# Value products of the grouped-query entry in three groups of tiles, and two weight splits pinned to other instructions

## The chip, the core and the metric

The kernel runs on one core of one Trainium2 chip. The metric is the device time of one execution in microseconds (us). A core has a matrix engine (TensorE, PE in the profile; PEld is its loading of weights), a vector engine (VectorE, DVE), an engine for activation functions (ScalarE, ACT), a general one (GpSimd, POOL) and one that only issues transfers (SyncE, SP). Each works through its own list of instructions in order; they wait for each other by semaphores. PE writes its products into PSUM, a memory of eight banks of 128 x 512 fp32 words; DVE and ACT read them from there into SBUF, the working memory. GpSimd doesn't read PSUM in this kernel.

## What is computed

One inference step of a two-layer diffusion backbone of width 1024, for 512 latent tokens and 128 context tokens that share all weights. The 640 tokens go through both layers side by side. Layer 0 has latent attention heads and neighbourhood attention heads, layer 1 has grouped-query attention; each is followed by a gated feed-forward block. The change lies at the start of layer 1's attention. Cut to what matters there:

```
def odd_project(h, w_in, q_norm, k_norm):
    p = h @ w_in
    q, k, v = jnp.split(p, [GQA_HEADS * GQA_HEAD_DIM, (GQA_HEADS + GQA_KV_HEADS) * GQA_HEAD_DIM], axis=-1)
    q = rms_norm(q.reshape(b, L, GQA_HEADS, GQA_HEAD_DIM), q_norm)
    k = rms_norm(k.reshape(b, L, GQA_KV_HEADS, GQA_HEAD_DIM), k_norm)
    ...
def odd_mixer_latent(h, c_k, c_v, w_in, q_norm, k_norm, w_out, cos, sin):
    q, k, v = odd_project(h, w_in, q_norm, k_norm)
    q = apply_rope(q, cos, sin)
    k = apply_rope(k, cos, sin)
    o = attend_blocked(q, jnp.concatenate([k, c_k], axis=1), jnp.concatenate([v, c_v], axis=1), GQA_SCALE)
    return o.reshape(b, L, -1) @ w_out
```

There are 8 query heads and 2 key/value heads of 128 columns each. The latent tokens read their own 512 keys and values and 128 cached ones; the context tokens read only themselves. Everything is fp32.

## The kernel before

**Precision and splits.** Every operand of a product is kept as two parts, a high part in PE's reduced fp32 form and a low part, the rest; a product is three matmuls (high x high, high x low, low x high). A weight of 128 x 1024 words is therefore loaded from memory into a raw buffer (three in turn) and split into one of three weight buffers: ACT copies the high part (line 184) and DVE subtracts it from the raw words to give the low part (line 185). The function is `unit` (line 175); its argument `behind` holds back ACT's half, DVE's half or both until a given instruction of the same engine has been issued. Names: wgk0 and wgk1 are the weights of the two key heads, wgv0 and wgv1 those of the values (the first and the second half of the 1024 inputs, for both heads), wgq0 to wgq7 those of the query heads; a trailing r is the raw buffer.

**Tokens and tiles.** The 640 tokens lie along the free dimension in two halves of 320 for keys and queries. For the values they are cut into five tiles of 128 tokens, each a product of 128 x 256 words (both value heads). The layer's input is h10 (h10h and h10l, its high and low part), eight blocks of 128 features.

**The entry.** Key head 0, query head 0 and the values are projected while the input is still being made block by block. `gvalues(ts, ks)` (line 1831) does the value products of the tiles `ts` for the feature blocks `ks`, the blocks in the outer loop, the tiles in the inner. The five tiles gvo[0] to gvo[4] lie in three PSUM banks, gvp0 to gvp2: tiles 0 and 1 in the first, 2 and 3 in the second, 4 in the third. The second half (line 2006) does all five tiles for blocks 4 to 7. Behind it, line 2011 splits each value tile and the tile of cached values cvf into gvh (ACT) and gvl (DVE); `valued` keeps the pair of instructions of the split that was written last. Line 2013 copies the context tokens' values to gvf, which GpSimd stores as an output. Then the second half of query head 0 is projected, and line 2016 closes the PSUM pool of the value banks and opens the one for the scores (`open_y(s=2)`, two tiles of two banks each).

**The heads.** For each query head the code builds named pieces and runs them in an order that is written out by hand. For head 0:

```
GQA_FIRST = "s0 x0 k0 k1 s1 r k2 k3 s2 k4 k5 s3 k6 k7 s4 q0 q1 q2 q3 q4 q5 q6 q7"
```

s0 to s4 are the score products (gs) of the five blocks of 128 queries, with the row maximum (gn) on DVE; x0 is the weighing of s0 (in the others it is part of the piece): a small product gb on DVE (line 1950), the Exp on ACT (line 1951), a reciprocal on DVE and the division on GpSimd (line 376). k0 to k7 are the products of key head 1 (gk1a, gk1b), r the query norms of head 0, q0 to q7 the query products of head 1. Each query product is followed by a copy out of PSUM (gqc), a square (gsq), a rotation on DVE (gqr, lines 1821 to 1824) and a split (gqh, gql).

**The order on each engine.** The order of the pieces fixes PE's order. The other engines' order is fixed by a planner of the framework when the program is built: it runs the program through estimates of its own and gives an engine that is free the next instruction that can start, by the order of the code where there are several. So an instruction that stands late in the code can run early, as wgq1's split does in the profile of before; `behind` is the code's means against that. Line 1894 pins head 1's query weights behind `valued[0]`, which in this version is the split of the cached tile.

Of the kernel before, what the change touches and what calls it, by code (L numbers as in the profile page):

```python
# [13 lines left out]
AF = mybir.ActivationFunctionType  # L14
ALU = mybir.AluOpType
# [5 lines left out]
KT = D // P  # L21
# [29 lines left out]
def body(ctx, tc, xT, vecs, crow, wm0, wm0g, wm1, wA, wNV, wNA, wMK, wMV, wOA, wGQ, wGK, wGV, wOC,  # L51
# [3 lines left out]
    V, S, G = nc.vector, nc.scalar, nc.gpsimd  # L55
# [32 lines left out]
    def bank(name, kind="m"):  # L88
        if kind == "m":
            return psp.tile([P, 512], F32, tag="m", bufs=4, name=name)  # L90
        return ypool["pool"].tile([P, 512], F32, tag=kind, bufs=ypool["tags"][kind], name=name)
# [10 lines left out]
    def tmp(name):  # L102
        return tp.tile([P, T], F32, tag="t", bufs=3, name=name)

    def f(ap):
        return ap.bitcast(F32)
# [41 lines left out]
    def vcol(i):  # L148
        return vec[:, i:i + 1]
# [12 lines left out]
    def load(src, n, name):  # L162
        raw = rawp.tile([P, 1024], F32, tag="raw", name=name)
        nc.sync.dma_start(raw[:, :n], src)
        return raw[:, :n]

    def after(inst, fn):
        if inst is None:
            return fn()
        with tc.issue_after(inst.ins):  # L170
            return fn()
# [3 lines left out]
    def unit(src, n, name, lo="v", pool=None, behind=None, raw=None):  # L175

        if raw is None:
            raw = load(src, n, name + "r")
        else:
            nc.sync.dma_start(raw, src)  # L180
        t = (pool or wp).tile([P, 2, 1024], F32R, tag="w", bufs=3, name=name)
        hi, lw = t[:, 0, :n], t[:, 1, :n]
        at = behind if isinstance(behind, tuple) else (behind, behind)
        split[:] = (after(at[0], lambda: S.activation(hi, raw, AF.Copy)),
                    after(at[1], lambda: (V if lo == "v" else G).tensor_tensor(lw, raw, f(hi), ALU.subtract)))
        return hi, lw
# [6 lines left out]
    def proj(ps, wh, wl, hh, hl, ks, c0, c1, first=True, last=True, w0=0):  # L193

        for j, k in enumerate(ks):
            a, b = wh[:, (w0 + j) * P:(w0 + j + 1) * P], wl[:, (w0 + j) * P:(w0 + j + 1) * P]
            mm3(ps[:, :c1 - c0], a, b, hh[k][:, c0:c1], hl[k][:, c0:c1], first and j == 0, last and j == len(ks) - 1)
# [280 lines left out]
    def lazy(fn):  # L478
        box = []

        def get():
            if not box:
                box.append(fn())
            return box[0]
        return get
# [176 lines left out]
    for r in range(2):  # L662
        hr, lr = STACK[r]
        src = ckf[hr, :512].rearrange("p (a b) -> p a b", b=P)
# [1146 lines left out]
    wk = {0: unit(wGK[0], 1024, "wgk0")}  # L1811
# [19 lines left out]
    def gvalues(ts, ks):  # L1831
        for k in ks:
            wh, wl = wv[k // 4]()
            a, b = wh[:, 256 * (k % 4):256 * (k % 4 + 1)], wl[:, 256 * (k % 4):256 * (k % 4 + 1)]
            for i in ts:
                c0, c1 = P * i, P * i + P
                PE.matmul(gvo[i], hh[k][:, c0:c1], a, start=k == 0 and i % 2 == 0, stop=False)
                PE.matmul(gvo[i], hh[k][:, c0:c1], b, start=False, stop=False)
                PE.matmul(gvo[i], hl[k][:, c0:c1], a, start=False, stop=k == KT - 1 and i in (1, 3, 4))
# [3 lines left out]
    def ksquare(v, c):  # L1843
        ksq[v, c] = tp.tile([P, HT], F32, tag="u", bufs=7, name=f"ksq{v}{c}")
        S.activation(ksq[v, c], kps[v, c], AF.Square)
# [27 lines left out]
    def keys(v, c, ks):  # L1873
        if 0 in ks:
            kbanks[v, c] = bank(f"gk{v}{'ab'[c]}")
            if c == 0:
                kns[v] = gp.tile([P, T], F32, name=f"kn{v}")
        if v not in wk:
            wk[v] = unit(wGK[v], 1024, f"wgk{v}")
        for k in ks:  # L1880
            proj(kbanks[v, c], *wk[v], hh, hl, [k], *HALF[c], first=k == 0, last=k == KT - 1, w0=k)
        if KT - 1 in ks:
            kps[v, c] = kbanks[v, c][:, :HT]
            if v == 0:
                ksquare(v, c)
            else:
                c0, c1 = HALF[c]
                S.activation(kns[v][:, c0:c1], kps[v, c], AF.Copy)
                kps[v, c] = kns[v][:, c0:c1]

    gqs, rope0, valued = {}, [], []

    def gqa_q(h):
        get = lazy(lambda: unit(wGQ[h], 1024, f"wgq{h}", behind=valued[0] if h == 1 else None))
        qh = gp.tile([P, T], F32R, tag="gqh", bufs=2, name=f"gqh{h}")
        ql = gp.tile([P, T], F32R, tag="gql", bufs=2, name=f"gql{h}")
        rq = tiny.tile([P, 5], F32, tag="rq", bufs=2, name=f"rq{h}")
        sq = tmp(f"gsq{h}")
        gqs[h] = qh, ql, rq
        out = []  # L1900
        for c, (c0, c1) in enumerate(HALF):
            def done(ps, c=c, c0=c0, c1=c1):
                qc = tp.tile([P, HT], F32, tag="u", bufs=7, name=f"gqc{h}{c}")
                S.activation(qc, ps[:, :HT], AF.Copy)
                S.activation(sq[:, c0:c1], qc, AF.Square)

                def turn(at=None):
                    qr = tp.tile([P, HT], F32, tag="u", bufs=7, name=f"gqr{h}{c}")
                    rope(qr, qc, vcol(V_GQ), c, f"gqr{h}{c}")
                    after(at, lambda: S.activation(qh[:, c0:c1], qr, AF.Copy))  # L1910
                    V.tensor_tensor(ql[:, c0:c1], qr, f(qh[:, c0:c1]), ALU.subtract)
                if h == 0 and c == 0:
                    rope0.append(turn)
                else:
                    turn()
            out += pieces_of(f"gq{h}{c}", qbank, get, hh, hl, list(range(KT)), c0, c1, done)

        def rstd(j0=0, j1=5):
            pr = bank(f"gr{h}")
            for j in range(j0, j1):  # L1920
                PE.matmul(pr[:, 2 * j:2 * j + 2], sq[:, P * j:P * j + P], ones[:, 0:2], start=True, stop=True)
            S.activation(rq[:, j0:j1], pr[:, 2 * j0:2 * j1].rearrange("p (a b) -> p a b", b=2)[:, :, 0], AF.Ln, bias=eps,
                         scale=1.0 / P)
            S.activation(rq[:, j0:j1], rq[:, j0:j1], AF.Exp, bias=lnsc, scale=-0.5)
        return out + [rstd]

    def gqa_scores(h, pts):
        v = h // 4
        ll = tiny.tile([P, 5], F32, tag="lg", bufs=4, name=f"gl{h}")

        def piece(j):
            qh, ql, rq = gqs[h]
            q = qh[:, P * j:P * j + P], ql[:, P * j:P * j + P]
            nm = tiny.tile([P, 1], F32, tag="nm", name=f"gn{h}_{j}")
            nb = tiny.tile([P, 1], F32, tag="nb", name=f"gb{h}_{j}")
            pss = bank2(f"gs{h}_{j}")
            if j < 4:
                pt = gp.tile([P, T], F32, tag="gp", bufs=8, name=f"gp{h}_{j}")
                scores(pss, q, kTh[v], kTl[v])
                V.tensor_reduce(nm, pss[:, :, :HT], AX.XY, ALU.max, negate=True)  # L1940
                src, dst, n = pss[:, :, :HT], halves(pt), T
            else:
                pt = gp.tile([P, P], F32, tag="gpp", bufs=1, name=f"gp{h}_{j}")
                src = pss[:, 0, :P]
                mm3(src, *q, kTh[v][:, 640:768], kTl[v][:, 640:768], True, True)
                V.tensor_reduce(nm, src, AX.X, ALU.max, negate=True)
                dst, n = pt, P

            def weigh():
                V.tensor_tensor(nb, nm, rq[:, j:j + 1], ALU.mult)  # L1950
                S.activation(dst, src, AF.Exp, bias=nb, scale=rq[:, j:j + 1], accum_out=ll[:, j:j + 1])  # L1951
                softmax_tail(pt, ll[:, j:j + 1], f"gr{h}_{j}", n)
                pts.append(pt)
            return weigh

        box = []
        rest = {f"s{j}": (lambda j=j: piece(j)()) for j in range(1, 5)}
        return {"s0": lambda: box.append(piece(0)), "x0": lambda: box[0](), **rest}
# [44 lines left out]
    knorm(0, 1, "k")  # L2003
    for v in range(2):
        ksplit(v, 512, 640, ckf[:, P * v:P * v + P])
    gvalues(range(5), range(4, KT))
    gvh = [gp.tile([P, 256], F32R, name=f"gvh{i}") for i in range(6)]
    gvl = [gp.tile([P, 256], F32R, name=f"gvl{i}") for i in range(6)]
    srcs = gvo[:4] + [cvf, gvo[4]]
    for i in (0, 1, 2, 3, 5, 4):  # L2010
        valued[:] = [(S.activation(gvh[i], srcs[i], AF.Copy), V.tensor_tensor(gvl[i], srcs[i], f(gvh[i]), ALU.subtract))]
    gvf = tmp("gvf")
    S.activation(gvf[:, :256], gvo[4], AF.Copy)
# [217 lines left out]
```

## Time and profile before

| | us |
|---|---|
| Time, median of 3 runs (lowest to highest) | 1493.63 (1492.7 to 1494.22) |
| The profiled execution's own time | 1493.43 |
| Its span, from the first to the last instruction | 1491.6 |
| PE busy | 1445.5 (97%) |
| DVE busy | 1210.0 (81%) |
| ACT busy | 763.3 (51%) |
| POOL busy | 207.8 (14%) |
| Mean granted clock of TensorE | 0.991 of full speed |

The profile's rows give the start, the duration, the engine, the line of the kernel, the operation and its names (written first, then "<-" and what is read, buffer numbers left out). "x2" are two like instructions merged. Brackets at the end give the idle time of the engine just before, and whose work ended it. All of PE's matmuls have line 63, since one helper issues them; they are told apart by names. Matmuls overlap in the pipeline, so their distance is read from their starts. The durations of several merged instructions are from the first start to the last end.

The entry of layer 1 lies at about 818 to 849 us of the span, head 0 at 851 to 870, the heads 1 to 7 up to about 1005. Layer 1's output projection and feed-forward block follow, up to the end.

### The profile page before, as it was taken

Reading aid. Unit: us, or ns where it says so; the run is one execution under the profiler, and the core shown is the slowest. Engines: PE = TensorE matmul, PEld = TensorE weight load, DVE = VectorE, ACT = ScalarE, POOL = GpSimd, SP = SyncE. Lnnn points to the kernel's source line nnn. Section 1 sums busy time; section 2 is a strip of 40 time slices with the busy share of each in tenths; the row PEclk is TensorE's granted clock in tenths of the full one; section 3 lists DMA queues with packets and bytes.
Section 4 is the critical chain, followed back from the end, with each engine's and each line's share of the span. In section 5 each row is a group of like instructions: output and inputs, shape, how many; then the busy total and the mean of one; then the engine's idle time right before and its main releaser. Section 6 shows DMA issues by size and latency. Waiting matters only on the chain.

```text
span 1491.6 us, 25707 instructions
## 1 busy us (share of the span) xinstructions
PE 1445.5 (97%) x9785; PEld 1395.5 (94%) x9785; DVE 1210.0 (81%) x2278; ACT 763.3 (51%) x1509; POOL 207.8 (14%) x298
## 2 busy tenths in 40 slices
PE   5999979999999999999999999999999999999996
PEld 4988968889999999999999999989999999999996
DVE  5786688985899999967998878775899999954496
ACT  5445577873755544441123666663755555542242
POOL 0325534432000000000001312222000000000000
PEclk9999989999999999999999999999999999999998
DMA  9544410105155555559864301004155556668521
GB/s 370 217 145 141 167 57 19 44 29 192 49 180 178 183 180 181 184 210 338 277 210 129 117 31 45 29 17 136 41 180 181 180 192 208 211 220 309 194 85 71
DMA packets 79899, 228.59 MB, mean 153 GB/s; under 512 B 8864, under 2 KB 14272, under 8 KB 79392
## 3 DMA queue, kind: packets, MB, share of 16 engines
q1 hardware_dynamic: 76544, 219.40, 43.0%
q0 software_dynamic: 1600, 5.14, 0.9%
q10 hardware_dynamic: 1632, 2.43, 0.5%
q8 instruction: 76, 1.25, 0.3%
q14 instruction: 47, 0.39, 0.1%
HBM read 192.23 MB, written 34.69 MB: 152 GB/s over the span
## 4 chain that ended last, share of the span: by engine, by line
PE 85%; DVE 7%; ACT 4%; DMA 2%; issue 2%; DVEq 0%; SPq 0%; ACTq 0%
PE fg L63 21%; PE fd L63 9%; PE fo L63 8%; PE fu L63 6%; PE gq L63 3%; PE nk L63 2%; PE nq L63 1%; PE fo_2b L63 1%; PE fo_0b L63 1%; PE gs L63 1%; PE fo_2a L63 1%; PE fo_0a L63 1%; PE go L63 1%; PE mod L63 1%; DMA mraw<-in_wm 1%
## 5 line engine op out<-in xcount | busy, mean ns | idle before, releaser
L1769 DVE SCALAR_TENSOR_TENSOR junk<-wm,cb 128x1024 bf16<-128x1024 f32 x62 | 75.6, 1220 | 5.7 <-DMA wm<-in_wm 5.1
L1221 ACT ACTIVATE sg<-g 128x320 f32<-128x320 f32 x34 | 16.0, 472 | 115.0 <-DVE g L1221 115.0
L63 PE MATMUL gq<-h10h,wgq 128*128 128x320 f32 x256 | 66.7, 318 | 0.0
L255 POOL TENSOR_SCALAR h10h<-h10t,gs,mods 128x320 fp32r<-128x320 f32 x4 | 3.6, 888 | 429.5 <-DVE h10t L249 427.8
L1221 DVE SCALAR_TENSOR_TENSOR junk<-wm,cb 128x1024 bf16<-128x1024 f32 x50 | 61.0, 1220 | 0.8
L1221 DVE TENSOR_TENSOR wY<-s,wY 128x1024 fp32r<-128x1024 f32 x40 | 48.8, 1219 | 1.3 <-ACT wY L1221 1.3
L1221 DVE TENSOR_TENSOR wZ<-s,wZ 128x1024 fp32r<-128x1024 f32 x40 | 48.8, 1220 | 0.0
L63 PEld LDWEIGHTS gq<-h10h,wgq 128*128 128x128 f32 x256 | 45.0, 188 | 0.9 <-PE gtp L67 0.2
L1221 ACT ACTIVATE wZ<-s 128x1024 fp32r<-128x1024 f32 x40 | 42.4, 1061 | 0.1
L1221 ACT ACTIVATE wY<-s 128x1024 fp32r<-128x1024 f32 x40 | 42.0, 1050 | 0.0
L1951 ACT ACTIVATE gp<-gs,gb,rq 128x640 f32<-128x640 f32 (+1 forms) x40 | 31.8, 796 | 16.7 <-DVE gb L1950 16.5
L63 PE MATMUL gq<-h10l,wgq 128*128 128x320 f32 x128 | 39.5, 308 | 0.0
L63 PE MATMUL fg<-h11E,wW 128*128 128x320 f32 x240 | 38.7, 310 | 0.0
L63 PE MATMUL fg<-h11q,wX 128*128 128x320 f32 x240 | 38.6, 309 | 0.0
L63 PE MATMUL fg<-h01q,wX 128*128 128x320 f32 x240 | 38.6, 309 | 0.0
L63 PE MATMUL fg<-h11N,wZ 128*128 128x320 f32 x240 | 38.6, 309 | 0.0
L63 PE MATMUL fg<-h01N,wZ 128*128 128x320 f32 x240 | 38.6, 309 | 0.0
L63 PE MATMUL fu<-h11q,wX 128*128 128x320 f32 x240 | 38.6, 309 | 0.0
L63 PE MATMUL fu<-h01q,wX 128*128 128x320 f32 x240 | 38.6, 308 | 0.0
L63 PE MATMUL fg<-h01E,wW 128*128 128x320 f32 x240 | 38.6, 309 | 0.0
L63 PE MATMUL fg<-h01C,wY 128*128 128x320 f32 x240 | 38.5, 309 | 0.0
L63 PE MATMUL fd<-h11q,wZ 128*128 128x320 f32 x240 | 38.5, 309 | 0.0
(3224 smaller groups left out, 5251.8 us busy)
## 6 DMA issues: line engine op xcount, KB each, us to landing
wm<-in_wm SPq DMA_DIRECT2D x48, 512.0 KB, 3.7
mraw<-in_wm SPq DMA_DIRECT2D x8, 1024.0 KB, 15.5
mraw<-in_wm SPq DMA_DIRECT2D x16, 512.0 KB, 3.7
hr_T<-sp_T SPq DMA_DIRECT2D x21, 320.0 KB, 5.6
hr_B<-sp_B SPq DMA_DIRECT2D x18, 320.0 KB, 6.4
mrow<-in_wm0g POOLq DMA_DIRECT2D x8, 512.0 KB, 6.6
wm<-in_wm0g SPq DMA_DIRECT2D x8, 512.0 KB, 3.4
x<-in_xT SPq DMA_DIRECT2D x8, 320.0 KB, 5.5
```

What stands on the lines that cost most here:

```text
L63: cls.last = nc.tensor.matmul(*a, **k)
L255: G.tensor_scalar(h[:, c0:c1], t, self.gsl[:, k, 0:1], self.ml[:, self.sh + k, 0:1], ALU.mult, ALU.add)
L1221: self.last = after(self.last, lambda: op(*a, **k))
L1769: def step(kind, at, line=lambda op, *a, **k: op(*a, **k)):
L1951: S.activation(dst, src, AF.Exp, bias=nb, scale=rq[:, j:j + 1], accum_out=ll[:, j:j + 1])
```

## The change

There are four edits.

1. The second half of the value products is done for tiles 0 and 1 first, then for 2 and 3, then for 4. Within a group the feature blocks stay in the outer loop.
2. The splits of the value tiles are written with the cached tile first and the last projected tile last, so that `valued` keeps the split of gvo[4].
3. The low half (DVE) of wgk1's split is pinned behind the DVE half of that split; its high half (ACT) stays free.
4. Both halves of wgq1's split are pinned behind the first weighing of head 0: ACT's half behind the Exp of s0, DVE's behind the product gb of s0. A new list, `weighed`, keeps those two instructions.

```diff
-            wk[v] = unit(wGK[v], 1024, f"wgk{v}")
+            wk[v] = unit(wGK[v], 1024, f"wgk{v}", behind=(None, valued[0][1]))
...
-    gqs, rope0, valued = {}, [], []
+    gqs, rope0, valued, weighed = {}, [], [], []
...
-        get = lazy(lambda: unit(wGQ[h], 1024, f"wgq{h}", behind=valued[0] if h == 1 else None))
+        get = lazy(lambda: unit(wGQ[h], 1024, f"wgq{h}", behind=weighed[0] if h == 1 else None))
...
             def weigh():
-                V.tensor_tensor(nb, nm, rq[:, j:j + 1], ALU.mult)
-                S.activation(dst, src, AF.Exp, bias=nb, scale=rq[:, j:j + 1], accum_out=ll[:, j:j + 1])
+                v = V.tensor_tensor(nb, nm, rq[:, j:j + 1], ALU.mult)
+                weighed.append((S.activation(dst, src, AF.Exp, bias=nb, scale=rq[:, j:j + 1], accum_out=ll[:, j:j + 1]), v))
...
-    gvalues(range(5), range(4, KT))
+    for ts in ((0, 1), (2, 3), (4,)):
+        gvalues(ts, range(4, KT))
...
-    for i in (0, 1, 2, 3, 5, 4):
+    for i in (4, 0, 1, 2, 3, 5):
         valued[:] = [(S.activation(gvh[i], srcs[i], AF.Copy), V.tensor_tensor(gvl[i], srcs[i], f(gvh[i]), ALU.subtract))]
```

In the last loop, index 4 is the cached tile and index 5 is gvo[4]. Key head 0's weights were split before this code, so the first line of the diff bears only on wgk1.

## The prediction

> **What bounds the kernel now.** I read the page first, then what TensorE (PE) waited for over the whole span, then the order in time of PE, VectorE (DVE) and ScalarE (ACT) around the changed lines. All times below are microseconds unless marked.
>
> ```profile
> PE 1445.5 (97%) x9785; PEld 1395.5 (94%) x9785; DVE 1210.0 (81%) x2278; ACT 763.3 (51%) x1509; POOL 207.8 (14%) x298
> ```
>
> PE is busy for 97% of the span, so an edit can pay only where PE stands still. The list of PE's waits shows where that is; here are the one at the changed lines and the two largest behind it:
>
> ```profile
> PE fn1p L63 <- DVE fn1acc L215: 2.6, 1, 2.6
> PE gs L63 <- DVE gvl L2011: 2.2, 1, 2.2
> ...
> PE gr L63 <- ACT gsq L1905: 0.8, 2, 0.6
> ```
>
> The second line is the place of the change: the first score product of head 0 (gs, piece s0) waited 2.2, once, for a split of a value tile (gvl, line 2011). Its PSUM pool opens when the pool of the three value banks closes, so every value tile has to be read out first. PE in order of time there:
>
> ```profile
> 848.73 0.31 PE L63 MATMUL gq<-h10l,wgq 128*128 128x320 f32 x1
> 848.87 0.31 PE L63 MATMUL gq<-h10h,wgq 128*128 128x320 f32 x1
> 851.40 0.53 PE L63 MATMUL gs<-gkh,gqh 128*128 128x320 f32 x2 [2.22 <-DVE gvl L2011]
> ...
> 852.36 0.31 PE L63 MATMUL gk1a<-h10h,wgk 128*128 128x320 f32 x1
> 852.51 0.30 PE L63 MATMUL gk1a<-h10l,wgk 128*128 128x320 f32 x1
> 852.65 0.46 PE L63 MATMUL gk1a<-h10h,wgk 128*128 128x320 f32 x2
> ...
> 863.00 0.36 PE L63 MATMUL gq<-h10h,wgq 128*128 128x320 f32 x1
> ```
>
> The matmuls follow each other at 0.15 (848.73 to 848.87), so s0 could have started at 849.02. By starts the hole is worth 851.40 - 849.02 = 2.38, by the idle time 2.22. Who fills it is on DVE and on ACT:
>
> ```profile
> 843.41 1.22 DVE L185 TENSOR_TENSOR wgk<-wgk1r,wgk 128x1024 fp32r<-128x1024 f32 x1
> 844.54 0.49 DVE L1911 TENSOR_TENSOR gql<-gqr,gqh 128x320 fp32r<-128x320 f32 x1
> ...
> 848.05 1.08 DVE L2011 TENSOR_TENSOR gvl<-gvp,gvh 128x256 fp32r<-128x256 f32 x3
> 849.69 1.23 DVE L185 TENSOR_TENSOR wgq<-wgq1r,wgq 128x1024 fp32r<-128x1024 f32 x1 [0.56 <-ACT wgq L184]
> 850.83 0.42 DVE L2011 TENSOR_TENSOR gvl<-gvp,gvh 128x256 fp32r<-128x256 f32 x1
> 851.17 0.54 DVE L1821 SCALAR_TENSOR_TENSOR gqr<-gqc,vec,tg 128x320 f32<-128x320 f32 x1
> ...
> 852.86 0.82 DVE L1940 TENSOR_REDUCE gn<-gs 128x1 f32<-128x640 f32 x1
> 853.61 0.48 DVE L1824 TENSOR_TENSOR gqr<-gqr,gqr01b 128x320 f32<-128x320 f32 x1
> ```
>
> ```profile
> 845.93 0.38 ACT L2011 ACTIVATE gvh<-gvp 128x256 fp32r<-128x256 f32 x1 [2.40 <-PE gvp L63]
> ...
> 848.58 1.07 ACT L184 ACTIVATE wgq<-wgq1r 128x1024 fp32r<-128x1024 f32 x1
> 849.53 0.40 ACT L2011 ACTIVATE gvh<-gvp 128x256 fp32r<-128x256 f32 x1
> 849.79 0.41 ACT L2013 ACTIVATE gvf<-gvp 128x256 f32<-128x256 f32 x1
> ...
> 850.24 0.47 ACT L1904 ACTIVATE gqc<-gq 128x320 f32<-128x320 f32 x1
> ```
>
> The reader is to see three things. The split of head 1's query weights (wgq1), not needed before 863.00, runs ahead of the last value tile on both engines. The low half of the key weights wgk1 (first needed by the third key product, 852.65) takes DVE at 843.41, while DVE is the engine that is late. And ACT stood idle for 2.40 until the first value tiles came, since all five finish together at the end.
>
> **The change part by part.** *Value products pair by pair.* The same 60 matmuls in another order: the bank of tiles 0 and 1 is complete after 24 of them, that of 2 and 3 after 48.
>
> ```profile
> 839.38 0.64 PE L63 MATMUL gvp<-wgv,h10h 128*128 128x256 f32 x2
> ...
> 846.69 0.29 PE L63 MATMUL gvp<-wgv,h10l 128*128 128x256 f32 x1
> ```
>
> 60 matmuls took 846.69 + 0.29 - 839.38 = 7.6, so with 24, 48 and 60 of them done the banks are complete at about 842.4, 845.5 and 847.0. PE's own time is unchanged: 0. The ACT copies of the first four tiles fall into the 2.40 that ACT sat idle. The last tile's copy (0.40), the state copy gvf (0.41) and its gvl (0.42) cannot start before 847.0, so ACT is through at 847.8 and gvl at 847.8: early enough.
>
> *The order of the splits.* The cache tile moves to the front; it needs no matmul, and the trace of before shows it done long ahead, so it costs nothing. What it changes is which pair stands in the variable "valued": the last projected tile's rather than the cache tile's, so that the pins mean something.
>
> *wgk1's low split behind the last gvl.* It leaves DVE before the value tiles: 844.54 - 843.41 = 1.13. *wgq1's split behind the first weighing of head 0* (on DVE the bias product, on ACT the Exp) removes 850.83 - 849.69 = 1.14 and the 0.56 that DVE waited there for ACT's half. Without the three, DVE's last gvl ends 2.83 earlier: 850.83 + 0.42 - 2.83 = 848.42. That is 0.6 ahead of 849.02; the cover is thin, and each microsecond of other DVE work planned in between would cost 0.4. With it, s0 starts at 849.02, at the earliest. **Sum: between 2.22 and 2.38; I take 2.3.**
>
> What is queued behind the new waits? wgk1's low half would run from 848.4 to 849.6. Its first user is the third key product, 852.65 - 851.40 = 1.25 behind s0's start, so at 850.27: 0.65 to spare. Later come wgq1's two halves (1.23 and 1.07), wanted at 863.00 - 2.3 = 860.7. The stretch from s0 to there is not full:
>
> ```profile
> 851.40:863.00 11.60, 11.60 (x82) 11.60 (x82) 7.49 (x17) 5.56 (x13) 2.38 (x3) 1.00 0.30 103
> ```
>
> DVE is busy 7.49 and ACT 5.56 of 11.60; with wgq1 added DVE has 8.7 and ACT 6.6. Nothing on PE waits for it. The two splits also free the buffers for two loads:
>
> ```profile
> 844.69 0.33 SPq L164 DMA_DIRECT2D wgq3r<-in_wGQ  x1
> 850.94 0.33 SPq L164 DMA_DIRECT2D wgq4r<-in_wGQ  x1
> ...
> wgq4r<-in_wGQ SPq DMA_DIRECT2D x1, 512.0 KB, 3.5
> ```
>
> ```profile
> 863.47 1.06 ACT L184 ACTIVATE wgq<-wgq3r 128x1024 fp32r<-128x1024 f32 x1
> ...
> 870.62 1.05 ACT L184 ACTIVATE wgq<-wgq4r 128x1024 fp32r<-128x1024 f32 x1
> ```
>
> They go out at about 849.7 and by 860 at the latest, and land 3.5 later, before 863.47 - 2.3 and 870.62 - 2.3. SP's queue holds only further loads of this kind behind them. Cost 0.
>
> One row speaks against moving splits towards GpSimd's (POOL's) work:
>
> ```profile
> L2011 DVE TENSOR_TENSOR gvl<-gvp,gvh x5: 415/418/419, 847.1 to 850.8; 128x256 fp32r<-128x256 f32 x5
> L2011 DVE TENSOR_TENSOR gvl<-gcvf,gvh x1: 1098/1098/1098, 831.1 to 831.1; 128x256 fp32r<-128x256 f32 x1
> ...
> 830.74 1.20 POOL L258 TENSOR_TENSOR h10l<-h10f,h10h 128x320 fp32r<-128x320 f32 x1
> ...
> 843.79 0.59 POOL L1861 DMA_DIRECT2D out_o_gkT<-kn  x1 [7.85 <-DVE kn L1859]
> ```
>
> The same split of 128x256 took 1098 ns beside a POOL sum and 418 ns without one, though its source was also another memory. So a collision may cost 0.68. But POOL's only work near 848.4 is the issue of the store of gvf, and under the issue at 843.79 wgk1's split kept its 1.22, so I add nothing; the bound is 0.68 against a margin of 0.65. The Trainium skill, GPSIMD Engine Reference, section 1 (Specifications), says that GpSimd shares its SBUF interfaces with VectorE and contends with its instructions that have two SBUF inputs; taken for the issue of a store too, it would make the sum 2.27 instead of 2.3, and the row at 843.79 does not bear that out.
>
> **Does the gain last to the end?** Behind 863 PE is busy nearly throughout:
>
> ```profile
> 886.00:1010.00 124.00, 123.16 (x823) 114.93 (x822) 97.61 (x214) 81.85 (x187) 29.66 (x33) 1.00 0.10 35
> 1010.00:1300.00 290.00, 289.40 (x1970) 288.63 (x1969) 263.00 (x432) 160.63 (x289) 12.79 (x8) 1.00 0.49 166
> ```
>
> Its waits there are for ACT and DVE results that follow from PE's own products (fn1p and gr in the list above, and less than 1 in all besides); none is for a load. So the whole schedule shifts. The profiled execution took 1493.43 around a span of 1491.6, the median of the runs is 1493.63, 0.2 above. 1493.43 - 2.3 = 1491.1; on the median's scale **1491.3**. About 0.2% (3.0) is what a measurement of this kernel can tell from no change, so the forecast gain lies within it.
>
> **The rivals.** *Another split takes the freed place.* The planner fills any hole with whatever is ready. Only wgq1 of the query units is pinned; wgq2's halves (1.1 and 1.2 like wgq1's) could go ahead of the last tile as wgq1's did. For it: the last value tile was held back 2.5 on ACT (847.0 to 849.53). Against: loads are issued in the order of the code, and wgq2 would need a weight buffer that wgq0 holds until 849. Time: no gain, 1493.6.
>
> *A new wait on wgk1.* If the last gvl ends after the query half gqc is ready (849.02 + 0.16 + 0.47 = 849.65, so 1.2 later than worked out), the turn of the query goes first: its first three instructions (852.86 - 851.17 = 1.69), the reduction of s0 (853.61 - 852.86 = 0.75), the sum (0.48), and only then wgk1 (1.22), ready at 853.8. s0 would start at 849.8, its key products would want wgk1 at 851.05: a stall of 2.7 against a remaining gain of 1.6. Time: 1.1 slower, 1494.7. The point is 849.65. Against it: DVE has no other work before 848.4. Were more weight splits to stand in front of the query's turn as well, each 1.2 more, it could reach 1497.
>
> *More than the hole.* The next stall is a query square held behind a weight split on ACT:
>
> ```profile
> 872.08 0.83 PE L63 MATMUL gr<-ones,gsq 128*128 128x2 f32 x6 [0.60 <-ACT gsq L1905]
> ```
>
> If the moved splits rearrange ACT so that it goes, and with it the 124.00 - 123.16 = 0.84 of heads 2 to 7, the gain is 2.9 to 3.7: 1490.7 to 1489.9. Nothing in the change aims at those; it would be an accident of the planner.
>
> **How the numbers follow.** The forecast gets 0.63, no gain 0.14, the new wait 0.11, more than the hole 0.12. The likeliest case's own range is 1490.9 to 1492.2 (a part of the 2.3 lost to one instruction of 0.4 to 0.9 in between). The range 1490.4 to 1494.0 takes in no gain and the nearer part of the larger gain, and leaves out the new wait and the largest gain. Faster by over 0.2% means below 1490.6: most of the last case and the lower edge of the forecast, 0.16. Slower by over 0.2% means above 1496.6: only the far end of the new wait, 0.05. The rest is 0.79.
>
> **What would show it.** Right: gs no longer waits for gvl, s0 follows the query products within 0.2; ACT copies the first two value tiles at about 842.5; wgk1's low half stands right behind the last gvl, and wgq1's behind the first bias product; every later piece lies 2.3 earlier. Wrong: a wait of gk1a for wgk1, a wgq2 split in front of the last value tile, a new wait of s2 for the exponentials of s0, or a stage behind 1010 that ends as late as now.

## The result and the profile after

The changed kernel takes 1490.53 us (median of 18 runs, 1489.16 to 1492.29), the one before 1493.69 beside it (18 runs, 1491.24 to 1496.46). The ratio is 0.9979, with a 95% interval of 0.9973 to 0.9986: 3.1 us faster (2.1 to 4.0), just over the 0.2% that the prediction took for what can be told from no change. One later run of the kernel before, at 1581.35, was in a slower state of the chip (granted clock 0.847) and is left out of the ratios and of the clocks averaged below. The profiled execution took 1490.9 around a span of 1489.1; the mean granted clock is 0.991 in both profiles.

Times below are in us. First PE in order of time at the start of head 0, after:

```profile
848.66 0.31 PE L63 MATMUL gq<-h10h,wgq 128*128 128x320 f32 x1
849.30 0.56 PE L63 MATMUL gs<-gkh,gqh 128*128 128x320 f32 x2 [0.33 <-ACT gvf L2014]
...
850.58 0.45 PE L63 MATMUL gk1a<-h10h,wgk 128*128 128x320 f32 x2
...
856.25 0.31 PE L63 MATMUL gk1b<-h10h,wgk 128*128 128x320 f32 x1
...
860.92 0.36 PE L63 MATMUL gq<-h10h,wgq 128*128 128x320 f32 x1
...
868.02 0.47 PE L63 MATMUL gs<-gkh,gqh 128*128 128x320 f32 x2
...
870.01 0.83 PE L63 MATMUL gr<-ones,gsq 128*128 128x2 f32 x6 [0.59 <-ACT gsq L1905]
```

The hole before s0 has shrunk from 2.22 to 0.33, but it has not closed, and another instruction ends it: gvf, ACT's copy of the context tokens' values. I measure it by starts, from the last query product to the first score product. This gap was 851.40 - 848.87 = 2.53 and is 849.30 - 848.66 = 0.64; matmuls that wait for nothing follow at 0.15. So **the change gains 1.89 here**. The third key product starts without a wait, so wgk1's low half came in time, and head 1 starts 863.00 - 860.92 = 2.08 earlier, 0.21 of which was there before the place of the change (848.87 to 848.66). The small stall of head 1's norms (gr, 0.59) is as it was.

ACT and DVE at the same place, after:

```profile
842.86 0.47 ACT L1910 ACTIVATE gqh<-gqr 128x320 fp32r<-128x320 f32 x1 [1.24 <-DVE gqr L1824]
843.24 0.36 ACT L2012 ACTIVATE gvh<-gvp 128x256 fp32r<-128x256 f32 x1
845.93 0.38 ACT L2012 ACTIVATE gvh<-gvp 128x256 fp32r<-128x256 f32 x1 [2.33 <-DVE gvl L2012]
...
846.80 0.36 ACT L2012 ACTIVATE gvh<-gvp 128x256 fp32r<-128x256 f32 x1
847.66 0.66 ACT L2012 ACTIVATE gvh<-gvp 128x256 fp32r<-128x256 f32 x2 [0.49 <-DVE gvl L2012]
...
848.86 0.38 ACT L2014 ACTIVATE gvf<-gvp 128x256 f32<-128x256 f32 x1
...
854.22 1.05 ACT L184 ACTIVATE wgq<-wgq1r 128x1024 fp32r<-128x1024 f32 x1
```

```profile
844.90 0.55 DVE L1823 SCALAR_TENSOR_TENSOR kro01b<-kn,ones,tg 64x320 f32<-64x320 f32 x1
845.47 0.42 DVE L2012 TENSOR_TENSOR gvl<-gvp,gvh 128x256 fp32r<-128x256 f32 x1
...
846.35 0.42 DVE L2012 TENSOR_TENSOR gvl<-gvp,gvh 128x256 fp32r<-128x256 f32 x1
...
847.21 0.42 DVE L2012 TENSOR_TENSOR gvl<-gvp,gvh 128x256 fp32r<-128x256 f32 x1
848.07 0.76 DVE L2012 TENSOR_TENSOR gvl<-gvp,gvh 128x256 fp32r<-128x256 f32 x2 [0.45 <-ACT gvh L2012]
848.75 1.22 DVE L185 TENSOR_TENSOR wgk<-wgk1r,wgk 128x1024 fp32r<-128x1024 f32 x1
...
855.30 1.23 DVE L185 TENSOR_TENSOR wgq<-wgq1r,wgq 128x1024 fp32r<-128x1024 f32 x1 [0.82 <-ACT wgq L184]
```

Here is what the prediction didn't see: **ACT and DVE take turns at a PSUM bank.** Tiles 0 and 1 share one, 2 and 3 another, gvo[4] has the third, from which gvf is read too. ACT copied tile 0 at 843.24 and then stood for 2.33, though tile 1's products had ended at about 842.3, until DVE had subtracted tile 0: DVE's first value difference ran from 845.47 to 845.89, and ACT's next copy started at 845.93. DVE was late because it had the keys' rotation to do (line 1823 up to 845.45). The same between tiles 2 and 3: difference until 847.63, copy at 847.66. And gvf started at 848.86, once the last difference had ended at 848.07 + 0.76 = 848.83. That is the rest of the hole: 848.83, a copy of 0.38 to 849.24, s0 at 849.30.

The Trainium skill, PSUM — Partial Sum Buffer, section "PSUM bank collisions raise a hardware error", says that two engines must not access the same bank and partitions at the same time, reads included, and that software has to order them. The trace agrees in that no two readers of a bank overlap: in the three cases just named ACT starts 0.03 to 0.04 behind the end of DVE's difference. What would happen if they did overlap, no run here shows.

The orders of instructions show the same for the kernel before, and correct the prediction. In the program as built the names keep their own numbers: gvh0 to gvh3 are the high parts of tiles 0 to 3, gvh5 that of gvo[4], gvl0 to gvl5 the low parts, and gvp0 to gvp2 the banks. ACT's and DVE's orders of before around the value splits, with other instructions left out at "...":

```
ACT  gvh0<-gvp0
...
ACT  gvh2<-gvp1
ACT  gvh1<-gvp0
ACT  gvh5<-gvp2
...
ACT  wgq1<-wgq1r
ACT  gvh3<-gvp1
ACT  gvf<-gvp2
...
DVE  gvl0<-gvp0,gvh0
...
DVE  gvl2<-gvp1,gvh2
DVE  gvl1<-gvp0,gvh1
DVE  gvl5<-gvp2,gvh5
DVE  wgq1<-wgq1r,wgq1
DVE  gvl3<-gvp1,gvh3
```

The tile that came last before the change was tile 3, not gvo[4]. Its copy had to follow tile 2's difference in the same bank; that left ACT a place, and the planner put wgq1's split into it. On the chip it was the fixed order that then held tile 3 back and no longer the bank: the first of the three differences of before at 848.05 is tile 2's, so it was over by about 848.47, and wgq1's copy began at 848.58. Outside the entry and head 0 the two kernels issue the same instructions in the same order on every engine.

### The profile page after: what moved, and what is told of

The parts are those of the page before. It is cut to its first block, busy times and chain, and to the rows that moved or that the text cites. A ratio compares the mean times of both kernels' runs of the same rounds, so it can differ in the third digit from the quotient of the medians.

```text
span 1489.1 us, 25707 instructions
## 1 busy us (share of the span) xinstructions
PE 1445.5 (97%) x9785; PEld 1395.5 (94%) x9785; DVE 1210.6 (81%) x2278; ACT 763.0 (51%) x1509; POOL 207.8 (14%) x298
## 4 chain that ended last, share of the span: by engine, by line
PE 85%; DVE 7%; ACT 5%; DMA 2%; issue 2%; DVEq 0%; SPq 0%; ACTq 0%
PE fg L63 21%; PE fd L63 9%; PE fo L63 8%; PE fu L63 6%; PE gq L63 3%; PE nk L63 2%; PE nq L63 1%; PE fo_0b L63 1%; PE fo_2b L63 1%; PE gs L63 1%; PE fo_2a L63 1%; PE fo_0a L63 1%; PE go L63 1%; PE mod L63 1%; PE fo_4b L63 1%
## 5 line engine op out<-in xcount | busy, mean ns | idle before, releaser
L63 PE MATMUL fd<-h01q,wZ 128*128 128x320 f32 x240 | 38.5, 309 | 0.0
```

Of the source, the lines that this page charges most:

```text
L63: cls.last = nc.tensor.matmul(*a, **k)
```

## The experiments

**How the traces are compared.** The beginning of the program, the same in all of these kernels, differs by up to 2.8 between executions: the last query product started between 846.10 and 848.87. So of each trace I take two numbers that are free of it: the gap from the start of the last query product to the start of gs, and the rest, from the start of gs to the end of the span.

| Kernel | gap | rest |
|---|---|---|
| before | 2.53 | 640.20 |
| after | 0.64 | 639.80 |
| after, second trace (e0) | 0.67 | 640.00 |
| pins, no grouping (e1; again e12) | 0.38; 0.37 | 639.73; 639.79 |
| grouping and new order of tiles, no pins (e2) | 1.16 | 639.86 |
| after without the pin of wgk1 (e3) | 0.87 | 639.75 |
| after without the pin of wgq1 (e4) | 1.08 | 640.12 |
| before with the pin of wgq1 alone (e5) | 0.75 | 639.81 |
| after, one copy for each bank (e7) | 0.15 | 639.29 |
| before, one copy for each bank (e9) | 1.24 | 639.75 |
| after, 2, 4, 6 idle products (e10, e11, e8) | 2.24; 4.32; 7.17 | 645.99; 641.58; 641.53 |

For before, the rest is 1491.6 - 851.40 = 640.20; the others likewise (spans are given to 0.1). In the first ten rows it stays within 639.7 to 640.2, but for e7, where another stall is gone.

**Which part makes the gain?** Four kernels with a part undone, one run each, and the kernel before beside them at 1492.69. Single times scatter by more than the effect (e2 below, with a larger gap than the changed kernel, took less time), so these are told apart by their gaps alone. Where an expectation speaks of a hole of 0.33 or 2.22, it means PE's idle time, which is less than the gap.

e1, the value products in one pass again, both pins and the order of tiles kept:

```diff
-    for ts in ((0, 1), (2, 3), (4,)):
-        gvalues(ts, range(4, KT))
+    gvalues(range(5), range(4, KT))
```

> The changed kernel with the value products back in one group of five tiles; the order of the splits and both pins stay. Theory A (the score products wait until the last value bank has been read out, and two readers of one bank go one after the other, so copy, difference, copy, difference of two tiles in a bank form a chain): all banks are complete only at the end, so the four copies no longer fit into ScalarE's idle time; score products start about 0.5 us after the last query product instead of 0.33 in the changed kernel, against 2.22 before. Theory B (the grouping is what closes the hole): the hole stays above 1.5 us.

Measured: 1490.22. Its PE in order of time:

```profile
848.29 0.31 PE L63 MATMUL gq<-h10h,wgq 128*128 128x320 f32 x1
848.67 0.53 PE L63 MATMUL gs<-gkh,gqh 128*128 128x320 f32 x2
```

The gap is 0.38, smaller than with the grouping, and the trace lists no wait. The grouping is not what closes the hole, so theory B fell; theory A was right about that, but had expected the gap to be larger than with the grouping.

e2, the reverse: grouping and new order of tiles, neither pin.

```diff
-            wk[v] = unit(wGK[v], 1024, f"wgk{v}", behind=(None, valued[0][1]))
+            wk[v] = unit(wGK[v], 1024, f"wgk{v}")
...
-        get = lazy(lambda: unit(wGQ[h], 1024, f"wgq{h}", behind=weighed[0] if h == 1 else None))
+        get = lazy(lambda: unit(wGQ[h], 1024, f"wgq{h}", behind=None))
```

> The changed kernel without both pins: the value products in three groups and the new order of the splits alone. Theory A: VectorE does the key weights' low half first, so its last value difference ends about 849.4 and ScalarE does the query weights' high half (1.07 us) ahead of the copy gvf, which reads the last bank: a hole of about 1.6 us. Theory B (the grouping closes the hole): about 0.3 us.

Measured: 1489.12, gap 1.16, a hole of 0.85, between the two numbers expected. ACT in order of time says why it is not 0.3:

```profile
845.38 0.64 ACT L2012 ACTIVATE gvh<-gvp 128x256 fp32r<-128x256 f32 x2
846.05 1.06 ACT L184 ACTIVATE wgq<-wgq1r 128x1024 fp32r<-128x1024 f32 x1
847.00 0.39 ACT L2014 ACTIVATE gvf<-gvp 128x256 f32<-128x256 f32 x1
```

wgq1's high half still gets in front of the last reader of the banks, now gvf. Its low half doesn't: with this order of tiles all value differences are done first, which is worth more than I had allowed.

e3 and e4 take one pin each away from the changed kernel (the first or the second pair of lines of e2's diff).

> The changed kernel without the pin on the key weights' low half. Theory A: that half returns to the front of VectorE's queue there and costs 1.13 us, less what PE still had in front of it: a hole of about 0.9 us instead of 0.33. Theory C (that pin does nothing, since VectorE had idle time to spare): 0.3 us.

> The changed kernel without the pins on head 1's query weights. VectorE's half then stands behind the last value difference and the key weights, where nothing of the banks waits; ScalarE's half stands in front of the copy gvf. Theory A (gvf, a reader of the last bank, releases the score products): a hole of about 0.9 us. Theory D (only the value differences on VectorE release them): 0.3 us.

Measured: e3 1491.3 with a gap of 0.87 (hole 0.56, halfway between its two theories), e4 1489.55 with 1.08 (hole 0.78, near theory A); in e4 wgq1's high half ran at 846.29 for 1.07, ahead of gvf at 847.24. In the changed kernel the pin of wgk1 is worth 0.23 and that of wgq1 0.44 of gap.

e5 goes the other way: the kernel before with wgq1's pin alone.

```diff
-        get = lazy(lambda: unit(wGQ[h], 1024, f"wgq{h}", behind=valued[0] if h == 1 else None))
+        get = lazy(lambda: unit(wGQ[h], 1024, f"wgq{h}", behind=weighed[0] if h == 1 else None))
```

> The kernel before with one edit: the split of wgq1 behind the first weighing of head 0. wgk1's low split stays ahead of the value tiles, the cache tile stays last in the list, and the products stay in one pass. From the last query product to gs (2.53 before, 0.38 with both pins and one pass, 0.87 with this pin and the grouping): theory A, the wgq1 pin is nearly all of it, since wgk1's low split takes VectorE before the first value tile is complete: 0.4 to 0.9. Theory B, the 1.13 of wgk1's low split push the value differences back one for one: 1.4 or more.

Measured: 1489.7, gap 0.75. One edit of the four closes 1.78 of the 1.89, with wgk1's split where it was. ACT copied one value tile at 844.40, three from 846.12, the last at 847.06, and gvf at 847.64; no weight split stood between them. So the parts replace one another, and their gains do not add up.

**Is it the shared bank?** e9 is the kernel before with none of the four edits. Instead each bank of two tiles is copied and subtracted as one piece of 128 x 512, so that no tile waits for its neighbour's difference. It computes the same.

```diff
-    for i in (0, 1, 2, 3, 5, 4):
-        valued[:] = [(S.activation(gvh[i], srcs[i], AF.Copy), V.tensor_tensor(gvl[i], srcs[i], f(gvh[i]), ALU.subtract))]
+    for h, l, src in ((gvh2[0], gvl2[0], gvb[0]), (gvh2[1], gvl2[1], gvb[1]), (gvh[5], gvl[5], gvo[4]), (gvh[4], gvl[4], cvf)):
+        valued[:] = [(S.activation(h, src, AF.Copy), V.tensor_tensor(l, src, f(h), ALU.subtract))]
```

> The kernel before, with one edit: the two value tiles of a bank are copied and subtracted as one piece of 512 columns. No pin, no new order of the products. Theory A (in the kernel before it was tile 3 that came last, held back because its copy had to wait for tile 2's difference in the same bank, and this let the query weights' split in front): that split now stands behind all value differences on VectorE. The last difference ends about 849.5 and gvf follows behind ScalarE's half of the split, at 850: a hole of about 1.0 us instead of 2.22. Theory E (the split goes ahead because it is ready first, whatever the banks): the hole stays at about 2.2 us.

Measured: 1491.13 (11 runs), ratio 0.9986 (0.9977 to 0.9995), gap 1.24. Its DVE in order of time:

```profile
846.61 0.68 DVE L2014 TENSOR_TENSOR gvl<-gvp,gvh 128x512 fp32r<-128x512 f32 x1
...
847.81 1.02 DVE L2014 TENSOR_TENSOR gvl<-gvp,gvh 128x512 fp32r<-128x512 f32 x2
849.18 1.23 DVE L185 TENSOR_TENSOR wgq<-wgq1r,wgq 128x1024 fp32r<-128x1024 f32 x1 [0.35 <-ACT wgq L184]
```

With no pin at all wgq1's low half now stands behind every value difference. So it was the turn-taking in tile 3's bank that had let it in, as theory A has it. (The edit also shortens the work a little, 0.60 and 0.68 for a whole bank against two copies of 0.38 and two differences of 0.42, and that share is not told apart.) The ACT half, at 848.08 ahead of gvf at 849.21, makes the 1.24 that are left.

**Can the rest be had?** e7 is the changed kernel with one copy for each bank, the last tile read out of PSUM once (gvf first, the split from gvf in SBUF), and ACT's half of wgq4 pinned behind head 1's last square, against the stall of 0.59 at gr. It computes the same.

```diff
+    for h, l, src in ((gvh[4], gvl[4], cvf), (gvh2[0], gvl2[0], gvb[0]), (gvh2[1], gvl2[1], gvb[1]), (gvh[5], gvl[5], gvf[:, :256])):
...
+        get = lazy(lambda: unit(wGQ[h], 1024, f"wgq{h}", behind=weighed[0] if h == 1 else (squared[1, 1], None) if h == 4 else None))
```

> The changed kernel with two additions. The two value tiles of a bank are copied and subtracted as one piece of 512 columns, and the last tile is read from PSUM once, into gvf, and split from there; and ScalarE's half of head 4's query weights is pinned behind the square of head 1's last query half. Theory A: the 0.33 us before the first score product go, and the 0.6 us before head 1's norm products go: 0.9 us less than the changed kernel, 2.8 us less than before (ratio about 0.9981 by the traces). Against it: the difference of a bank in one piece starts later, and the split of head 4's weights may delay another copy.

Timed beside it, the changed kernel itself once more:

> The changed kernel once more, as a measure of how far two measurements of the same pair differ. Theory 1 (the gain is the closed hole and nothing else; the two traces show 1.9 us of it): ratio 0.9987, an end that is 1.9 us earlier. Theory 2 (there is a second gain that the traces of single executions don't show): ratio 0.9979 again, 3.1 us.

Measured with 11 runs each, and the kernel before at 1493.08: e7 1490.06, ratio 0.9976 (0.9967 to 0.9985); after 1490.34, ratio 0.9983 (0.9974 to 0.9992). The second measurement of the changed kernel thus lies between the two ratios expected, and does not decide between its theories. In e7's trace both stalls are gone: s0 follows at 0.15, and the norms run as ten matmuls in one piece.

```profile
848.46 0.31 PE L63 MATMUL gq<-h10h,wgq 128*128 128x320 f32 x1
848.61 0.45 PE L63 MATMUL gs<-gkh,gqh 128*128 128x320 f32 x2
...
868.24 1.17 PE L63 MATMUL gr<-ones,gsq 128*128 128x2 f32 x10
```

By trace it is 1.0 better than after (0.49 of gap, 0.51 of rest); by time 0.3, which these runs cannot tell from nothing.

e12 times the pins without the grouping:

> The changed kernel with the value products in one pass of all five tiles again, so the order of the splits and the two pins alone, timed. Theory A, the pins make the whole gain and the grouping makes none: ratio to the kernel before 0.9975 to 0.9985, from the last query product to gs about 0.4. Theory B, the single trace of this kernel was lucky and the grouping is worth some tenths: 0.9990, and a distance over 0.7.

Measured with 8 runs, and the kernel before at 1493.73: 1490.2, ratio 0.9976 (0.9966 to 0.9987), gap 0.37. As theory A has it, the pins and the order of tiles make the whole gain. The grouping adds none that can be measured; by trace it costs 0.27 of gap.

**What does a hole cost?** Idle products on DVE before the last value difference make the hole longer at will; the outputs are the same.

```diff
     for i in (4, 0, 1, 2, 3, 5):
-        valued[:] = [(S.activation(gvh[i], srcs[i], AF.Copy), V.tensor_tensor(gvl[i], srcs[i], f(gvh[i]), ALU.subtract))]
+        for n in range(6 if i == 5 else 0):
+            d = after(d or valued[0][1], lambda: V.tensor_tensor(dose, tg[:, 0, :], tg[:, 1, :], ALU.mult))
+        valued[:] = [(S.activation(gvh[i], srcs[i], AF.Copy), after(d, lambda: V.tensor_tensor(gvl[i], srcs[i], f(gvh[i]), ALU.subtract)))]
```

Six of them (e8), then four (e11) and two (e10):

> The changed kernel with six products of 128x640 into an unused tile on VectorE (0.7 us each) in front of the last value difference, which adds idle work and changes no result. The planner mixes them with the rotation of the query's second half, so the last difference comes about 5.9 us later. Theory 1 (a hole on PE at this place moves the end by as much): the first score product 5.8 us later, the time 5.8 us longer than the changed kernel's, about 3.9 us longer than before. Theory 3 (part of a hole here is made up later): the end moves by less than 4 us.

> The changed kernel with four idle products on VectorE ahead of the last value difference. From the last query product to gs: 0.64 + 4 x 0.82 + up to three rotation steps of 0.5, so 3.9 to 5.4. In the run with six products the granted clock was 0.50 for 3.2 behind a hole of 6.86, which cost about 1.6 more than the hole. If a hole of this length already lowers the clock: clock 0.50 for the first 3.2 behind it, first two gs products 0.90 instead of 0.56, and the rest of the span grows by the hole and 1.6 more. If not: clock 1.00, and it grows by the hole alone.

> The changed kernel with two idle products of 128x640 on VectorE ahead of the last value difference (0.82 each in the run with six). From the start of the last query product to the start of gs it took 0.64 in the changed kernel, 2.53 in the one before; with two products, and perhaps one rotation step of 0.55 between them, it should be 2.3 to 2.9. Theory 1, a hole here moves the whole rest of the program by its size and by nothing else: the end of the span minus the start of the last query product is 640.6 plus 1.7 to 2.3, so 642.3 to 642.9, as before the change (642.73), the granted clock stays at 1.00 behind the hole, and the time is that of the kernel before: ratio 0.9995 to 1.0002. Theory 2, part of the gain is from the new order of the splits behind the hole: 641.5 or less and a ratio of 0.999 or less with the same hole.

Measured: e8 1498.5, ratio 1.0037 (1.0024 to 1.0049); e11 1496.03 in a single run; e10 1496.21, ratio 1.0018 (1.0008 to 1.0028). The smallest dose made a hole shorter than that of the kernel before, and yet a kernel slower than it; theory 1 of e10 fell, and theory 2 with it. In e8 the gap grew by 6.53 and the time by 8.2 over the changed kernel's: more than theory 1's hole alone, and the opposite of theory 3. e11's gap of 4.32 is in the range expected, and its clock fell. The next three views are PE of e10 in order of time, then the granted clock by windows of e10 and of e11 (the columns are the window and its length, then busy time of PE, PEld, DVE, ACT and POOL, the clock, the share and rate of DMA).

```profile
847.97 0.31 PE L63 MATMUL gq<-h10h,wgq 128*128 128x320 f32 x1
850.21 0.56 PE L63 MATMUL gs<-gkh,gqh 128*128 128x320 f32 x2 [1.93 <-ACT gvf L2017]
...
851.42 0.47 PE L63 MATMUL gk1a<-h10l,wgk 128*128 128x320 f32 x1
852.64 0.90 PE L63 MATMUL gk1a<-h10h,wgk 128*128 128x320 f32 x2 [0.75 <-DVE wgk L185]
...
862.40 0.31 PE L63 MATMUL gk1b<-h10h,wgk 128*128 128x320 f32 x1
```

```profile
850.20:851.20 1.00, 0.99 (x7) 0.99 (x8) 0.97 (x2) 0.00 (x0) 0.54 (x1) 1.00 0.00 0
851.20:861.40 10.20, 9.45 (x38) 9.05 (x37) 5.27 (x11) 3.70 (x8) 1.16 (x2) 0.50 0.19 66
861.40:870.00 8.60, 8.60 (x61) 8.60 (x60) 5.57 (x11) 5.05 (x10) 2.02 (x3) 1.00 0.41 123
```

```profile
852.70:855.60 2.90, 2.88 (x11) 2.88 (x12) 2.85 (x5) 0.47 (x1) 0.54 (x1) 0.50 0.13 45
855.60:861.00 5.40, 5.40 (x39) 5.40 (x39) 2.97 (x8) 3.52 (x9) 0.80 (x1) 0.99 0.31 100
```

Two things came on top of the hole. One is **the stall on wgk1**, the mechanism of the prediction's second rival, and e10's DVE shows it: the last difference now ends behind the query half's copy, so the query's rotation goes first and wgk1's split comes three instructions later.

```profile
849.32 0.42 DVE L2015 TENSOR_TENSOR gvl<-gvp,gvh 128x256 fp32r<-128x256 f32 x1
849.66 0.54 DVE L1821 SCALAR_TENSOR_TENSOR gqr<-gqc,vec,tg 128x320 f32<-128x320 f32 x1
...
850.78 0.55 DVE L1823 SCALAR_TENSOR_TENSOR gqr01b<-gqc,vec,tg 64x320 f32<-64x320 f32 x1
851.36 1.23 DVE L185 TENSOR_TENSOR wgk<-wgk1r,wgk 128x1024 fp32r<-128x1024 f32 x1
```

The other is **the granted clock**: behind the hole it stood at 0.50, for 10.2 in e10, 2.9 in e11 and 3.3 in e8 (in the last two it had fallen during the hole). From the start of gs to the first product of gk1b it takes 856.25 - 849.30 = 6.95 in after, 862.40 - 850.21 = 12.19 in e10: 5.24 more. Of this 0.75 is PE's idle time at the stall and the rest, 4.5, the clock (4.1, if the stall is taken as the 1.15 by which the third key product came later). In e11 the same stretch took 8.29, in e8 8.39: 1.3 to 1.4 more. That is most of the 1.7 to 1.8 by which the rest of e11 and e8 stands over after's. e10's profiled execution (1498.01) was the slowest of its nine, so its 10.2 is not the usual figure.

**What stays open.** The gap accounts for 1.89 of the gain, the traces from the last query product on for 2.3 and 2.1, the medians for 3.2 and 2.7. The intervals of the two measurements, 2.1 to 4.0 and 1.2 to 3.9, both hold the 2.3, so scatter alone may be the difference. One reading would close it: if the clock sometimes falls behind the hole of before too, in executions that were not traced. Each execution lists its mean granted clock, rounded to 0.001. Over 42 of before these average 0.9918, over 29 of after 0.9929 (standard errors 0.0002 each). As means over a span of 1490, at a clock of 0.50 where it is low, 0.0010 is 3.1 more at half clock, up to 1.5 of lost time; with the 1.89 that gives up to 3.4. The same working fits e10: its nine average 0.9906, 6.9 more at half clock than after, 3.4 of lost time; the ratios leave 5.8 - 1.6 (gap) - 0.75 (stall) = 3.5.

A mean does not say where the clock was low, though. It was 0.991 in the trace of after and 0.993 in e0's, the same kernel, and the difference comes from the first 220 us, with five stretches of 3.41 at half clock in one trace and three in the other. The last section works out from all traces when the clock falls: before's hole of 2.22 would then cost the clock in about two executions of three, 0.9 on average, and 1.89 + 0.9 = 2.8 is close to the medians. But the one trace of before has 1.00 behind the hole, so this is an estimate and not shown.

## Why the prediction was right, point by point

**The bound and the place: right.** PE's hole before s0 was where the gain lay, and in the first ten rows of the table the rest behind it stays the same within 0.5 (e7 apart), as "the whole schedule shifts" had it; head 1 started 2.08 earlier, for the 2.3 forecast. No new PE wait appeared, and head 1's stall at gr (0.59), which the third rival would have removed, stayed.

**Which tile was last: wrong.** The working took the last projected tile for the one that was held back on ACT ("held back 2.5 on ACT (847.0 to 849.53)"). It was tile 3, put behind its neighbour in the bank. The time of the wait was read rightly, the cause not: the names without buffer numbers do not tell the tiles apart.

**"ACT is through at 847.8 and gvl at 847.8: early enough": the step that failed.** It treated ACT's copies and DVE's differences as free of each other once the tile is complete. They alternate in each bank, and gvf, in gvo[4]'s bank, had to follow the last difference: it ended at 849.24 instead of 847.8 (847.6 on this trace, which is 0.21 ahead at this place), and 0.49 of the hole stayed. The sign "s0 follows the query products within 0.2" was missed, with 0.64. DVE's sum (2.83, last difference over at 848.42) had the right terms for DVE's own work, but not the 0.45 that DVE then waited for copies which had waited for DVE. It ended at 848.83.

**The grouping: costed at nothing, rightly; its benefit was imagined.** "The ACT copies of the first four tiles fall into the 2.40 that ACT sat idle" is wrong: ACT copied one tile, at 843.24 behind a query split, and was idle for 2.33 all the same, waiting for DVE. The sign of two copies at about 842.5 did not appear.

**The two pins: right.** wgk1's low half ran at 848.75 to 849.97, right behind the last difference; its first user started at 850.58, 0.61 later (0.65 was worked out). It ran beside the issue of gvf's store on POOL for part of that time and took its 1.22, so the 0.68 for a collision, and the sum of 2.27 that went with it, found no support:

```profile
849.54 0.54 POOL L2015 DMA_DIRECT2D out_o_gv<-gvf  x1 [5.37 <-ACT gvf L2014]
```

wgq1's halves ran behind the first bias product and Exp, at 854.22 and 855.30, 4.4 ahead of head 1. What the prediction had not seen is that wgq1's pin alone closes nearly as much of the gap (e5).

**The rivals.** Another split in the freed place: not with the pins; without wgq1's pin it is wgq1's own ACT half that stands ahead of gvf (e2, e4). The new wait on wgk1: its mechanism is real (e10), with the point where it was worked out, but it cost 0.75 rather than 2.7, since the reduction of s0 and the sum did not go first, and the change keeps clear of it. The point was the end of the query half's copy: after's last difference ended at 848.83, that copy at 849.57; in e10 the difference ended at 849.74, 0.99 behind the copy (848.31 + 0.44).

**The size, and luck.** The sum of 2.3 measured 1.89 at the gap. The time came out 0.8 below the forecast of 1491.3, inside the range but only 0.13 above its lower edge, and below the likeliest case's own range (1490.9 to 1492.2). It even lies in the range of the third rival, *more than the hole* (1490.7 to 1489.9), though nothing of that rival's mechanism happened. So the place and the pins were foreseen, and that the number fits as well as it does is partly luck: the hole gave 0.4 less than the sum, and the medians gave more than the hole. The prediction took the hole's price to be its length; the runs with idle products show that a hole here can cost more than that. The gain of 0.21% lies on the edge between the cases "same", where most of the chance was, and "faster" (below 1490.6, with a chance of 0.16), and the interval takes in both.

## What to carry to other kernels

When two engines read tiles that share a PSUM bank, count their instructions as one chain, copy, difference, copy, difference, and not as two streams; one copy of the whole bank, or one read and the rest from SBUF, takes the chain apart. Before an edit of several parts is kept, undo them one at a time: here one pin closes 1.78 of the 1.89 by itself, and the regrouping of the products closes nothing. A hole on TensorE is to be priced at its length and what the clock may lose behind it, and with a hole of this size one trace does not show whether it does.

## What the runs showed of the hardware

**The clock is set anew every 3.41 us, by how busy PE was in the 3.41 us before.** In all fourteen traces every change of the granted clock lies on a grid of 3.41. Cut on that grid, here are two stretches of before and then four of e10, with the columns as above (PE's busy time is the first of the engines'; its ends are modelled, so the shares are rough):

```profile
846.50:849.91 3.41, 2.68 (x20) 2.42 (x19) 2.72 (x9) 2.73 (x9) 0.00 (x0) 1.00 0.28 112
849.91:853.32 3.41, 1.92 (x13) 1.95 (x14) 3.35 (x6) 2.11 (x6) 0.54 (x1) 1.00 0.43 130
```

```profile
847.80:851.21 3.41, 1.48 (x11) 1.21 (x10) 3.35 (x7) 1.59 (x4) 0.54 (x1) 1.00 0.00 0
851.21:854.63 3.42, 2.67 (x10) 2.27 (x10) 2.95 (x6) 0.79 (x2) 0.00 (x0) 0.50 0.36 119
854.63:858.04 3.41, 3.41 (x16) 3.41 (x15) 0.73 (x1) 0.65 (x2) 0.00 (x0) 0.50 0.20 78
858.04:861.45 3.41, 3.41 (x14) 3.41 (x15) 1.59 (x5) 2.26 (x5) 1.21 (x2) 0.50 0.00 0
```

The grid cut before's hole of 2.22 in two, at 849.91: PE was busy for 0.79 of the first stretch and 0.56 of the second, and the clock stayed. All of e10's 1.93 fell into one stretch, which left PE busy for 0.43 of it, and the next three ran at 0.50. (The stall of 0.75 came after the fall.) Over all stretches at full clock in the fourteen traces, the next one was at half clock in 36 of 36 cases where PE had been busy for up to 0.52, in 6 of 15 from 0.53 to 0.59, and in none of the 5877 from 0.60 on. A stretch at half clock brought full clock back in 34 of 35 cases where PE was busy for 0.88 or more, and in none of 21 up to 0.79 (three lie between); the one exception is e10's at 854.63, and its cause is open.

From these figures an estimate of what a hole does on an otherwise busy PE: up to 1.4 of idle time (0.40 of 3.41) leaves the clock alone, and from 1.6 (0.475 of 3.41) within one stretch lowers it. A hole of 2.22 placed at random on the grid has 1.6 in one stretch in (3.41 + 2.22 - 2 x 1.62) / 3.41 = 0.70 of the cases. At 1.3 to 1.4 for a stretch at half clock, as in e11 and e8, that is 0.9 on average.

The Trainium skill, TensorE: Matmul & The Clock Gate, "Part 1: The HAM clock gate", gives a free-running window of about 3.4 us, an idle one of which lowers the clock to half and a busy one of which restores it, and its rule is no idle gap over about 3.4 us. The grid and the two clocks agree with it, and so do the holes of 4.01 (e11) and 6.86 (e8). The rule on gaps is not a safe bound here: in e10 no gap reached even 2 us, since a window need only be about half idle.

**The beginning of the program varies by up to 2.8** between executions of the same instructions, more than the gain of the whole change. Part of this goes with the clock: in the first 220 us the traces have from two (e4) to five stretches of 3.41 at half clock, and the four traces that reach the last query product latest (848.46 to 848.87) are the four with five. A difference of single spans says little here; the distance between two instructions around the change says much.
